# A hybrid decoder block: two more Strassen tiles in another product order, block sums moved into the last loop, GpSimd's order changed

## The chip, the cores and the metric

One core of a Trainium2 chip runs the whole block. The metric is the device time of one execution in microseconds (us), less being better.

## The reference

One decoder block on 512 tokens of width 1024, in float32, cut to what matters here:

```python
h = rmsnorm(x, attn_norm_g)
q, k_c, v_c, k_s, v_s, k_w, v_w, nsa_gate, rwkv_in, gate_a, gate_b = split(h @ w_in)
o_a = nsa_mixer(q, k_c, ..., cmp_w1_k, cmp_w2_k, ...)   # 8 heads; compressed, selected, window branches
o_b = rwkv7_mixer(rwkv_in, ...)                         # 8 heads of 64, a recurrence over the tokens
x = x + (sigmoid(gate_a) * (o_a @ w_proj_a) + sigmoid(gate_b) * (o_b @ w_proj_b)) @ w_out
u = rmsnorm(x, ffn_norm_g) @ w_up                       # 1024 -> 2 * 2816, a gate half and a value half
val, gate = split(conv_b + causal_conv3(u))             # per channel, width 3
x = x + (silu(gate) * val) @ w_down                     # 2816 -> 1024
```

## The kernel before

TensorE multiplies fp32r numbers, and every float32 operand is split into a high and a low part (`hh`, `hl` of the activations; `whi`, `wlo` of a weight, which is loaded to `raw`, rounded by ScalarE to `whi`, and subtracted by VectorE or GpSimd to `wlo`). A product is then three matmuls: hh·whi, hl·whi and hh·wlo.

The program runs through these stages: the input projection; the RWKV recurrence over eight chunks c = 0 to 7, with the key compression of the attention woven into it (TensorE's and GpSimd's order there is that of the code); the attention, whose gaps are filled with tiles of `w_proj_b`; the merge, eight column tiles of `w_proj_a`, one in 2.7 us; `w_out`; the second norm; the FFN up; the FFN down.

**FFN up.** The 22 column tiles f of 128 gate and 128 value columns are either dense (48 matmuls of 512 columns, both halves together) or, for f in `SF` = 3 to 17, done with Strassen's seven products of half size (`up_strassen`): `up_product` is 12 matmuls of 256 columns. Five products use block sums of the input (`R1`, `M2`, `R3`, `Q`) and four of them block sums of the weights (`TS1` to `TS4`). The PSUM banks are `mmb()`, `pa()` and `pb()` (names `ps_mm`, `ps_a`, `ps_b` in the profile). The gate's first half is H11 + H12: each is a product in a bank of its own, ScalarE copies H11 to `us`, and VectorE adds the bank of H12 to it. The convolution `conv` then reads the gate from `cr` in SBUF.

**Sums of weights.** They are made in HBM by DMAs that GpSimd issues: `sums_in_memory` copies rows of `w_up` to `usum` and adds others with an accumulating DMA, one row block k of 128 rows and all columns of `SF` at a time. These have a width of 128 x 15 = 1920 columns (7680 bytes); `max_dma_last_dim=2048` bounds the bytes of one packet, so that the accumulating ones are issued as 128x4x480 (512 packets of 1920 bytes), and a sum of sums as 480x512 (480 packets of 2048 bytes). The copies and adds are started one by one during the recurrence, and the rest when the attention begins. `down_sums` does the same for `w_down` (`dsum`): `down_copy` and `down_add`, each started by `after`, in which GpSimd waits for a named result with a copy to `hold`. All DMAs of GpSimd share one queue, q0 in the profile; SP's weight loads go through q1.

**FFN down.** Strassen as well; the first `PD` = 9 pairs of tiles have their block sums made in `gate_value`, during the FFN up, and `down_tokens` makes the others in steps. In the last, joint loop over g = 0 to 10 the products P4, P5, P7 and P1 run together.

**Keys of the compression.** `kv_proj(1, n)` ends with `norm_keys(1)`, four multiplications `QK<-QK,kss` on GpSimd, which wait for `kss` from VectorE. Behind them in GpSimd's order stand the loads of `spent_load(3, 0)`: the compression weights into buffers that earlier work has used up (`AB`, `BKT`, `AR`).

The lines of the weight loads, `norm_keys` and the spent loads:

```python
def spent_load(s4, a): ...          # AB, BKT, AR <- in_cmp_w_k, on GpSimd's queue
            if c == 1:
                spent_load(3, 0)
            ...
            if c:
                memory_down.send(Xs[0:1, 0, 0:1])    # the next down_copy or pair of down_adds
            if 2 <= c < 7:
                next(memory_sums)                    # the next copy to usum; at the end all adds
```

Of the kernel before, what the change touches and what calls it, by code (L numbers as in the profile page):

```python
# [10 lines left out]
F32 = mybir.dt.float32  # L11
# [21 lines left out]
DOWN_ = [range(g, min(g + 2, NG)) for g in range(0, NG, 2)]  # L33
NCMP = 31
# [4 lines left out]
SF = range(3, 18)  # L39
# [45 lines left out]
def hybrid_block(ctx: ExitStack, tc: tile.TileContext, A: dict, out: bass.AP):  # L85
# [152 lines left out]
    def sums_in_memory(early=5, lead=3):  # L238
        todo = [(t, s_ - e, ij, src) for s_ in range(6)
                for t, e, ij, src in ((TS1, 0, (0, 0), (0, 1)), (TS3, 0, (0, 1), (1, 1)), (TS2, 1, (1, 1), TS1),  # L240
                                      (TS4, 2, (1, 0), TS2)) if 0 <= s_ - e < 4]
        todo[12:14] = todo[13], todo[12]

        def copy(n):
            t, k, ij, _ = todo[n]
            nc.gpsimd.dma_start(usum[t][128 * k:128 * k + 128], up_rows(*ij, k))

        def addition(n):
            t, k, _, src = todo[n]
            nc.gpsimd.dma_start(usum[t][128 * k:128 * k + 128],  # L250
                                up_rows(*src, k) if type(src) is tuple else usum[src][128 * k:128 * k + 128],
                                accum_op=ALU.add, max_dma_last_dim=2048)

        for n in range(early):
            copy(n)
            yield
        for n in range(early - lead):
            addition(n)
        for n in range(early, len(todo) + lead):
            if n == len(todo):  # L260
                yield
            if n < len(todo):
                copy(n)
            addition(n - lead)
# [15 lines left out]
    def down_sums():  # L280
        for g in range(NG):
            after((yield))
            down_copy(g)
        for g in range(0, NG, 2):
            after((yield))
            for g_ in range(g, min(g + 2, NG)):
                down_add(g_)
        while True:
            yield
# [4 lines left out]
    def weight_tiles():  # L294
# [48 lines left out]
        for f in list(SF) + [None]:  # L343
            p = SF[-1] if f is None else f - 1
            if f is not None:
                stream += [up_block(f, 0, 0), up_block(f, 1, 0)]
            if f != SF[0]:
                stream.append(up_sum(p, TS4))
            if f is not None:
                stream.append(up_sum(f, TS2))  # L350
            if f != SF[0]:
                stream.append(up_block(p, 1, 1))
            if f is not None:
                stream += [up_sum(f, TS1), up_sum(f, TS3)]
# [513 lines left out]
    def kv_proj(b, n):  # L868
# [8 lines left out]
        if b == 1:  # L877
            norm_keys(1)
# [64 lines left out]
    with tc.manual_schedule(engines={mybir.EngineType.PE, mybir.EngineType.Pool}):  # L943
        for m in range(NGA):
            act(siga[m], dense_fm(hh, hl))
        below(0)
# [3 lines left out]
        left(0)  # L950
        left(16)
# [179 lines left out]
    with tc.manual_schedule(engines={mybir.EngineType.PE, mybir.EngineType.Pool}):  # L1131
# [7 lines left out]
        for c in range(NCH):  # L1139
# [451 lines left out]
    cr = fp.tile([128, 3, 512], F32, name="cr", tag="d1b")  # L1591
# [45 lines left out]
    def down_tokens():  # L1637
# [23 lines left out]
        for a, b, N, t in tails:  # L1661
# [5 lines left out]
    craw = [cr[:, 0], cr[:, 1], cr[:, 2], cgq[:, 14:16].rearrange("p a n -> p (a n)")]  # L1667
# [30 lines left out]
    def up_strassen():  # L1698
# [4 lines left out]
        for f in list(SF) + [None]:  # L1703
            if f is not None:
                B1 = mmb()[:, b0]
                up_product(B1, H[0][0], True, 1 if f == SF[0] else 2)
                u = [us[:, 3 * (f % 2) + k] for k in range(3)]
                Cg, Cv = craw[f % 2], craw[2 + f % 2]
# [7 lines left out]
            if prev is not None:  # L1716
                urgent.clear()
                f_, B1_, B5_, u_, Cg_, Cv_ = prev
                up_product(B1_, H[1][1])
                act(Cg_[:, b1], B1_)  # L1720
                cg = conv(Cg_, NF + f_, f_ % 2)
            if f is not None:
                up_product(B1, M2)
                act(u[1], B1, AF.Copy, scale=-1.0)
            if prev is not None:
                up_product(B5_, Q)
                stt(Cv_[:, b0], B5_, -1.0, u_[1])
                cv = conv(Cv_, f_, 2 + f_ % 2)
                gate_value(f_, cg, cv)
            if f is not None:  # L1730
                B5 = pb()[:, b0]
                up_product(B5, R1, True)
                up_product(B1, R3)
                act(u[2], B1, AF.Copy, scale=-1.0)
                stt(Cv[:, b1], B5, -1.0, u[2])
                prev = f, B1, B5, u, Cg, Cv
# [123 lines left out]
    with tc.manual_schedule(engines=everything):  # L1860
# [13 lines left out]
        for i, gs in enumerate(DOWN_):  # L1874
# [12 lines left out]
            elif i == 3:  # L1887
                assert next(side, 0) == 0
# [6 lines left out]
            for j, g in enumerate(gs):  # L1895
                product(P1, (a1[:, 0, g], a1[:, 1, g]), [x[:, j] for x in w], g == 0, g == NG - 1)
        u = [[x[:, o + 2 * t:o + 2 * t + 2].rearrange("p a n -> p (a n)") for t in range(2)]
             for x, o in ((cgq, 8), (cgq, 12), (ql, 12))]
# [93 lines left out]
```

## Time and profile before

| | |
|---|---|
| time, median of 3 runs | 800.53 us (799.17 to 800.59) |
| the profiled execution | 801.03 us, of which the span is 799.2 us |
| TensorE busy | 786.7 us, 98% of the span |
| VectorE, ScalarE, GpSimd busy | 633.0, 486.6, 116.0 us (79%, 61%, 15%) |
| DMA | 146.47 MB, mean 183 GB/s; q1 37.1% and q0 27.5% of 16 engines' time |
| the accumulating and copying DMAs into `usum` | 32 issues of 960 KB, about 30 us from issue to landing |

The profiled execution is 1.83 us longer than its span, and 0.50 us above the median. TensorE works nearly all the time, so what counts is how much work it has and where it is made to wait.

### The profile page before, as it was taken

The page shows a single profiled execution, that of the slowest core. Times are in us where ns is not written, and L with a number is a line of the kernel's source. Part 1 is how long each engine was busy: PE and PEld are TensorE (multiplying, and loading weights), DVE is VectorE, ACT ScalarE, POOL GpSimd, SP SyncE. Part 2 cuts the span into 40 slices and gives each one's busy share as a digit, 9 for nine tenths or more (in the row PEclk, how much of TensorE's full clock was granted, in tenths as well). Part 3 has the DMA queues.
Part 4 walks back from the last instruction along what each step waited for, and adds up shares of the span by engine and source line. Part 5 has one row for each costly group of instructions (what it writes and reads, how often), then busy time and mean ns, then how long its engine had stood idle before and what let it go on. Part 6 is the DMA issues. An engine that isn't in the chain of part 4 may idle for free.

```text
span 799.2 us, 14545 instructions
## 1 busy us (share of the span) xinstructions
PE 786.7 (98%) x5547; PEld 672.4 (84%) x5547; DVE 633.0 (79%) x1177; ACT 486.6 (61%) x928; POOL 116.0 (15%) x165
## 2 busy tenths in 40 slices
PE   7999999998999999999999999999999999999998
PEld 5788888886778788788788898999999988888886
DVE  4688899973565588889595489999999999899766
ACT  6777765553355578778444356777777775554442
POOL 5311121153121052120000100000000000003101
PEclk9999999999999999999999999999999999999999
DMA  7554533337999679999857933666666642585753
GB/s 222 152 162 154 178 95 111 80 107 198 208 211 257 192 143 262 273 257 275 213 161 261 198 135 107 198 185 176 192 182 181 184 144 66 164 304 204 251 178 110
DMA packets 149402, 146.47 MB, mean 183 GB/s; under 512 B 6398, under 2 KB 125365, under 8 KB 149205
## 3 DMA queue, kind: packets, MB, share of 16 engines
q1 hardware_dynamic: 128592, 85.57, 37.1%
q0 software_dynamic: 19680, 57.44, 27.5%
q10 hardware_dynamic: 1060, 2.55, 1.0%
q8 instruction: 43, 0.70, 0.4%
q14 instruction: 27, 0.21, 0.1%
HBM read 140.09 MB, written 47.38 MB: 235 GB/s over the span
## 4 chain that ended last, share of the span: by engine, by line
PE 95%; DMA 2%; DVE 1%; ACT 1%; issue 0%; POOL 0%; SPq 0%; DVEq 0%; ACTq 0%; POOLq 0%
PE ps_mm L126 52%; PE ps_mm L1682 11%; PE ps_mm L1798 6%; PE ps_b L1682 5%; PE ps_a L126 5%; PE ps_a L1798 4%; PE ps_b L1798 4%; PE ps_a L1682 3%; PE ps_b L126 2%; PE ps_b L1408 1%; DMA raw<-in_w_in_dram 1%; PE ps_mm L1408 1%; DMA AB<-in_cmp_w_k_dram 1%; DMA kc<-in_consts_dram 1%; PE ps_b L449 0%; ACT whi L129 0%
## 5 line engine op out<-in xcount | busy, mean ns | idle before, releaser
L129 ACT ACTIVATE whi<-raw 128x1024 fp32r<-128x1024 f32 (+2 forms) x153 | 152.7, 998 | 120.9 <-PE ps_mm L126 49.0
L411 DVE TENSOR_TENSOR wlo<-raw,whi 128x1024 fp32r<-128x1024 f32 (+1 forms) x138 | 158.5, 1150 | 43.0 <-ACT whi L129 23.4
L126 PE MATMUL ps_mm<-hh,whi 128*128 128x512 f32 (+1 forms) x384 | 149.2, 392 | 0.3 <-ACT whi L129 0.2
L126 PE MATMUL ps_mm<-hl,whi 128*128 128x512 f32 (+1 forms) x384 | 141.8, 382 | 0.0
L126 PE MATMUL ps_mm<-hh,wlo 128*128 128x512 f32 (+1 forms) x384 | 95.9, 381 | 0.0
L126 PEld LDWEIGHTS ps_mm<-hh,whi 128*128 128x128 f32 x384 | 72.3, 188 | 16.9 <-issue 1.5
L126 PEld LDWEIGHTS ps_mm<-hh,wlo 128*128 128x128 f32 x384 | 72.2, 188 | 14.0
L126 PEld LDWEIGHTS ps_mm<-hl,whi 128*128 128x128 f32 x384 | 70.3, 188 | 13.3 <-DVE hl L141 0.3
L1830 POOL DMA_DIRECT2D cgq<-dsum x6 | 3.2, 541 | 270.2 <-DVE ql L132 234.1
L129 ACT ACTIVATE P<-P,nm 128x512 f32<-128x512 f32 (+3 forms) x64 | 35.3, 554 | 8.0 <-DVE nm L1371 7.9
L141 DVE SCALAR_TENSOR_TENSOR cgq<-cr,cw,cgq 128x511 f32<-128x511 f32 (+1 forms) x44 | 32.9, 747 | 5.0 <-ACT cgq L129 4.5
L1371 DVE CUSTOM_DVE_ANT_0 P<-ps_a,AB 128x512 f32<-128x512 f32 (+3 forms) x64 | 29.4, 483 | 2.1 <-PE ps_a L126 2.1
L1682 PE MATMUL ps_mm<-hl,whi 128*128 128x256 f32 x120 | 30.1, 283 | 0.0
L1682 PE MATMUL ps_mm<-hh,whi 128*128 128x256 f32 x120 | 30.1, 283 | 0.0
L132 DVE TENSOR_TENSOR cgq<-cgq 128x512 f32<-128x512 f32 (+1 forms) x36 | 24.2, 671 | 1.5 <-DMA cgq<-in_w_down_dram 0.9
L1682 PEld LDWEIGHTS ps_mm<-hl,whi 128*128 128x128 f32 x120 | 23.0, 192 | 0.1
L1682 PEld LDWEIGHTS ps_mm<-hh,whi 128*128 128x128 f32 x120 | 23.0, 192 | 0.1
L129 ACT ACTIVATE QK<-ps_mm 128x64 f32<-128x64 f32 (+5 forms) x52 | 13.3, 302 | 15.3 <-PE ps_mm L126 15.3
L126 PE MATMUL ps_mm<-whi,hh 128*128 128x280 f32 (+2 forms) x72 | 22.4, 331 | 0.0
L126 PE MATMUL ps_mm<-whi,hl 128*128 128x280 f32 (+2 forms) x72 | 21.9, 323 | 0.0
L129 ACT ACTIVATE ring<-cgq 128x1024 fp32r<-128x1024 f32 x12 | 12.7, 1059 | 14.8 <-issue 5.4
L141 DVE SCALAR_TENSOR_TENSOR cgq<-ps_mm,cw,cgq 128x511 f32<-128x511 f32 (+1 forms) x28 | 20.3, 741 | 0.2
(544 smaller groups left out, 2022.5 us busy)
## 6 DMA issues: line engine op xcount, KB each, us to landing
usum<-in_w_up_dram POOLq DMA_DIRECT2D x24, 960.0 KB, 30.3
raw<-in_w_in_dram SPq DMA_DIRECT2D x38, 512.0 KB, 5.3
raw<-usum SPq DMA_DIRECT2D x60, 256.0 KB, 3.4
raw<-in_w_up_dram SPq DMA_DIRECT2D x45, 256.0 KB, 3.4
dsum<-in_w_down_dram POOLq DMA_DIRECT2D x22, 512.0 KB, 5.7
raw<-in_w_down_dram SPq DMA_DIRECT2D x20, 512.0 KB, 4.6
usum<-usum POOLq DMA_DIRECT2D x8, 960.0 KB, 27.6
raw<-in_w_up_dram SPq DMA_DIRECT2D x14, 512.0 KB, 3.8
```

Source lines behind the costliest of these rows:

```text
L126: te.matmul(o, lhsT=l, rhs=r, start=start, stop=stop)
L129: sc.activation(o, i, f, **kw)
L132: v.tensor_tensor(o, a, b, op=op)
L141: v.scalar_tensor_tensor(o, a, s, b, op0=op0, op1=op1)
L411: eng.tensor_tensor(lo, raw, hi.bitcast(F32), op=ALU.subtract)
L1371: v.tensor_tensor_reduce(out=P[:, b, r], in0=sp[:, r - r0, b], in1=BT[:, h, 384 - 128 * qt:512], scale=-1.0, scalar=-NEG, op0=ALU.add, op1 ...
L1408: te.transpose(pt[:, 128 * i:128 * i + 128], P[:, x, i, 128 * k:128 * k + 128], ident)
L1682: te.matmul(bank_, lhsT=(hi, lo)[k // 4][:, k % 4], rhs=y[:, k % 4], start=first and k == 0 and y is x[0], stop=k == 7, skip_group_check=n ...
L1798: te.matmul(banks[t], lhsT=x_[:, 128 * t:128 * t + 128], rhs=y, start=first and n == 0, stop=end and n == 2, skip_group_check=more)
L1830: nc.gpsimd.dma_start(raws[g][i], s_)
```

## The change

Three things. (1) `SF` is 3 to 19, 17 tiles in place of 15, and the seven products of a tile are done in another order: H11, then R1 and the H22 of the tile before, M2, H12, Q of the tile before, R3. From the third tile on ScalarE writes H11 into the bank `G`, H12 is accumulated on top of it, and the convolution reads the gate from that bank; VectorE's addition is gone there. `usum` becomes 2176 columns wide. (2) `PD` is 10, and the block sums of the other pairs in `down_tokens` and `two_parts` are made later, partly in the joint loop. (3) GpSimd: `norm_keys(1)` stands after `spent_load(3, 0)`; the first two `down_copy` are started before the recurrence; the additions of `dsum` start singly at first; six copies to `usum` in place of five stand ahead of the attention's bulk.

```diff
-SF = range(3, 18)
+SF = range(3, 20)
+DOWN_SUMS = [[0], [1]] + [range(g, min(g + 2, NG)) for g in range(2, NG, 2)]
...
-    def sums_in_memory(early=5, lead=3):
+    def sums_in_memory(early=6, lead=3):
...
             act(vt[:, t, b], bkv[t][:, 128:256])
             if b == 1:
                 act(gts[:, t], bkv[t][:, 256:280], AF.Tanh, scale=0.5)
-        if b == 1:
-            norm_keys(1)
...
         for m in range(NGA):
             act(siga[m], dense_fm(hh, hl))
+        memory_down.send(siga[0][0:1, 0:1])
         below(0)
...
         left(0)
+        memory_down.send(ABq[0][0:1, 0, 32:33])
         left(16)
...
             if c == 1:
                 spent_load(3, 0)
+                assert next(kv1, 0) == 0
+                norm_keys(1)
...
-            if c:
+            if c > 1:
                 memory_down.send(Xs[0:1, 0, 0:1])
-            if 2 <= c < 7:
+            if c > 1:
                 next(memory_sums)
...
-                act(u[0], B1)
-                B2 = pa()[:, b0]
-                up_product(B2, H[0][1], True)
-                tt(Cg[:, b0], u[0], B2, ALU.add)
+                G = pa()
+
+                on_top = f > SF[0] + 1
+                act(G[:, b0] if on_top else us[:, 4 + f % 2], B1)
...
+                B5 = pb()[:, b0]
+                up_product(B5, R1, True)
+                Cv = craw[f_ % 2]
+                stt(Cv[:, b1], B5, -1.0, u_[1])
                 up_product(B1_, H[1][1])
-                act(Cg_[:, b1], B1_)
-                cg = conv(Cg_, NF + f_, f_ % 2)
+                act(G_[:, b1], B1_)
+                cg = conv(G_, NF + f_, f_ % 2)
             if f is not None:
                 up_product(B1, M2)
-                act(u[1], B1, AF.Copy, scale=-1.0)
+                act(u[0], B1, AF.Copy, scale=-1.0)
+                up_product(G[:, b0], H[0][1], not on_top)
+                if not on_top:
+                    tt(G[:, b0], G[:, b0], us[:, 4 + f % 2], ALU.add)
...
             elif i == 4:
-                two_parts(a2b[:, 0, :, 0], a2b[:, 1, :, 0], cgq[:, 8:14])
+                next(side)
...
-                if g in (2, 4, 6):
-                    k = g // 2 - 1
-                    two_parts(a1[:, 0, k], a1[:, 1, k], q4[k])
-                if g == NG - 2:
+                if g < 3:
+                    next(side)
+                elif g == 3:
+                    assert next(side, 0) == 0
+                    two_parts(a2b[:, 0, :, 0], a2b[:, 1, :, 0], cgq[:, 8:14])
+                elif g == 7:
+                    two_parts(a1[:, 0, 0:3], a1[:, 1, 0:3], ql[:, 0:3])
+                elif g == NG - 2:
                     two_parts(a1[:, 0, 3:7], a1[:, 1, 3:7], ql[:, 3:7])
```

GpSimd's order in the first chunks of the recurrence, where `wlo` are low parts of input weights, `QK` the normed queries and keys, and `AB`, `BKT`, `AR` the spent loads. Before:

```order
L411 TENSOR_TENSOR wlo<-raw,whi 128x840 x2
L411 TENSOR_TENSOR wlo<-raw,whi 128x560
L883 TENSOR_TENSOR QK<-QK,kss 128x128 x4
L956 TENSOR_TENSOR QK<-QK,qss 128x512 x4
L883 TENSOR_TENSOR QK<-QK,kss 128x128 x4
L915 DMA AB<-in_cmp_w_k_dram 128x4x256
L913 DMA BKT<-in_cmp_w_k_dram 128x256 x2
L913 DMA AR<-in_cmp_w_k_dram 128x2x128 x2
L270 COPY hold<-Xs 1x1
L276 DMA dsum<-in_w_down_dram 256x1x512 x2
```

And now:

```order
L412 TENSOR_TENSOR wlo<-raw,whi 128x840
L271 COPY hold<-sg_1716 1x1
L277 DMA dsum<-in_w_down_dram 256x1x512
L412 TENSOR_TENSOR wlo<-raw,whi 128x840
L271 COPY hold<-AB 1x1
L277 DMA dsum<-in_w_down_dram 256x1x512
L412 TENSOR_TENSOR wlo<-raw,whi 128x560
L882 TENSOR_TENSOR QK<-QK,kss 128x128 x4
L957 TENSOR_TENSOR QK<-QK,qss 128x512 x4
L914 DMA AB<-in_cmp_w_k_dram 128x4x256
L912 DMA BKT<-in_cmp_w_k_dram 128x256 x2
L912 DMA AR<-in_cmp_w_k_dram 128x2x128 x2
```

The second four multiplications `QK<-QK,kss` now follow these rows; the spent loads have moved ahead of them, and two transfers of `dsum` with their waits ahead of two of the `wlo`.

GpSimd's order at the start of the attention, where the bulk of the weight sums is issued. Before:

```order
L250 DMA usum<-in_w_up_dram 128x4x480 x2
L246 DMA usum<-in_w_up_dram 128x1920
L250 DMA usum<-in_w_up_dram 128x4x480
L246 DMA usum<-in_w_up_dram 128x1920
L250 DMA usum<-in_w_up_dram 128x4x480
L246 DMA usum<-in_w_up_dram 128x1920
L250 DMA usum<-usum 480x512
```

And now:

```order
L251 DMA usum<-in_w_up_dram 128x8x272 x3
L247 DMA usum<-in_w_up_dram 128x2176
L251 DMA usum<-in_w_up_dram 128x8x272
L247 DMA usum<-in_w_up_dram 128x2176
L251 DMA usum<-usum 544x512
```

An accumulating transfer from `w_up` was cut into 4 packets of 480 columns for each of 128 rows, and is now cut into 8 of 272; one copy more lies ahead of these rows. The rows go on in the same pattern.

## Rows read from the trace of the kernel before

**Rows 1.** The page's chain that ended last, shares of the span.

```profile
PE 95%; DMA 2%; DVE 1%; ACT 1%; issue 0%; POOL 0%; SPq 0%; DVEq 0%; ACTq 0%; POOLq 0%
```

**Rows 2.** Windows: stretch, us, busy PE, PEld, DVE, ACT, POOL, granted clock, DMA, GB/s.

```profile
495.40:643.70 148.30, 148.30 (x1237) 148.30 (x1236) 137.14 (x199) 108.51 (x169) 0.00 (x0) 1.00 0.63 183
720.20:780.00 59.80, 59.80 (x266) 49.51 (x265) 45.91 (x50) 27.36 (x32) 10.97 (x15) 1.00 0.61 207
195.00:200.00 5.00, 4.38 (x20) 2.49 (x21) 0.00 (x0) 0.00 (x0) 1.45 (x2) 0.66 1.06 243
```

**Rows 3.** The chain that ended last: start, us, engine, tile, line, count.

```profile
190.90 4.68 DMA AB<-in_cmp_w_k_dram
...
496.79 1.44 PE ps_a L1682 x12
...
649.29 40.83 PE ps_mm L126 x180
```

**Rows 4.** TensorE's timeline, recurrence: start, us, operation, [idle before and its releaser].

```profile
172.85 0.81 PE L126 MATMUL ps_mm<-wlo,hh 128*128 128x280 f32 x5
...
183.63 0.58 PE L126 MATMUL ps_a<-UV,AB 128*64 128x64 f32 x14
...
195.62 0.46 PE L126 MATMUL ps_mm<-AB,sg 128*64 128x256 f32 x1 [2.44 <-DMA AB<-in_cmp_w_k_dram]
```

**Rows 5.** GpSimd's timeline, the recurrence.

```profile
169.51 1.36 POOL L411 TENSOR_TENSOR wlo<-raw,whi 128x560 fp32r<-128x560 f32 x1 [5.01 <-ACT whi L129]
...
189.48 1.48 POOL L883 TENSOR_TENSOR QK<-QK,kss 128x128 f32<-128x128 f32 x4 [9.65 <-DVE kss L141]
...
194.31 2.14 POOL L276 DMA_DIRECT2D dsum<-in_w_down_dram  x2
```

**Rows 6.** ScalarE's timeline, around 170 us and in the merge.

```profile
170.54 0.59 ACT L129 ACTIVATE AB<-ps_a 32x512 f32<-32x512 f32 x1 [1.94 <-PE ps_b L126]
...
398.40 0.63 ACT L129 ACTIVATE whi<-raw 128x512 fp32r<-128x512 f32 x1 [3.33 <-DMA raw<-in_w_proj_a_dram]
...
400.19 0.63 ACT L129 ACTIVATE whi<-raw 128x512 fp32r<-128x512 f32 x1 [0.63 <-DMA raw<-in_w_proj_a_dram]
```

**Rows 7.** VectorE's timeline, one Strassen tile.

```profile
566.30 0.41 DVE L132 TENSOR_TENSOR cr<-us,ps_a 128x256 f32<-128x256 f32 x1
```

**Rows 8.** VectorE's groups after 640 us: count | busy, mean ns | idle before.

```profile
L132 DVE TENSOR_TENSOR a2b_pairs<-cgq,a2b_pairs 128x1536 fp32r<-128x1536 f32 x1 | 1.8, 1758 | 0.4 <-ACT a2b_pairs L129 0.4
...
L132 DVE TENSOR_TENSOR ql<-ql,a2a_pairs 128x1280 f32<-128x1280 f32 x1 | 1.5, 1485 | 0.0
```

**Rows 9.** DMA queues from 290 to 400 us: packets, MB, share of 16 engines.

```profile
q0 software_dynamic: 8370, 23.73, 89.7%
```

**Rows 10.** The same from 324 to 326 us: accumulating packets alone.

```profile
q0 software_dynamic: 205, 0.42, 113.9%
```

**Rows 11.** The same from 57 to 58 us: plain packets of 512 bytes.

```profile
q1 hardware_dynamic: 634, 0.32, 108.0%
```

**Rows 12.** The same from 413 to 414 us: plain packets of 2048 bytes.

```profile
q1 hardware_dynamic: 185, 0.37, 98.7%
```

**Rows 13.** The same from 384 to 391 us, the first loads of the merge.

```profile
q0 software_dynamic: 531, 1.70, 91.5%
q1 hardware_dynamic: 521, 0.26, 17.1%
```

**Rows 14.** The same from 393 to 400 us.

```profile
q0 software_dynamic: 90, 0.17, 12.8%
```

**Rows 15.** SP's timeline: two issues of merge weights.

```profile
387.04 0.37 SPq L382 DMA_DIRECT2D raw<-in_w_proj_a_dram  x1
...
394.00 0.37 SPq L382 DMA_DIRECT2D raw<-in_w_proj_a_dram  x1
```

**Rows 16.** TensorE's timeline, two of the merge's eight tiles.

```profile
400.33 1.98 PE L126 MATMUL ps_mm<-oaT,whi 128*128 128x512 f32 x8
...
403.05 1.98 PE L126 MATMUL ps_mm<-oaT,whi 128*128 128x512 f32 x8
```

More of the change, by code (lines that the diff above doesn't have):

```diff
@@ L283, in down_sums @@
             down_copy(g)
-        for g in range(0, NG, 2):
+        for gs in DOWN_SUMS:
             after((yield))
-            for g_ in range(g, min(g + 2, NG)):
-                down_add(g_)
+            for g in gs:
+                down_add(g)
         while True:
@@ L345, in weight_tiles @@
             if f is not None:
-                stream += [up_block(f, 0, 0), up_block(f, 1, 0)]
+                stream.append(up_block(f, 0, 0))
             if f != SF[0]:
-                stream.append(up_sum(p, TS4))
+                stream += [up_sum(p, TS1), up_sum(p, TS4)]
             if f is not None:
-                stream.append(up_sum(f, TS2))
+                stream += [up_sum(f, TS2), up_block(f, 1, 0)]
             if f != SF[0]:
@@ L353, in weight_tiles @@
             if f is not None:
-                stream += [up_sum(f, TS1), up_sum(f, TS3)]
+                stream.append(up_sum(f, TS3))
         yield stream[:1], 4, 128, v
@@ L1590, in hybrid_block @@
     R3Q = xr.tile([128, 2, 2, 4, 256], F32R, name="R3Q", tag="x1")
-    cr = fp.tile([128, 3, 512], F32, name="cr", tag="d1b")
+    cr = fp.tile([128, 2, 512], F32, name="cr", tag="d1b")
     us = fp.tile([128, 6, 256], F32, name="us", tag="d3a")
@@ L1660, in down_tokens @@
             yield
-        for a, b, N, t in tails:
             stt(ql[:, a:b], N, -1.0, whole(t[:, 0, 0:b - a, 0]), ALU.mult, ALU.subtract)
@@ L1665, in down_tokens @@
             yield
-    craw = [cr[:, 0], cr[:, 1], cr[:, 2], cgq[:, 14:16].rearrange("p a n -> p (a n)")]
+    craw = [cr[:, 0], cr[:, 1]]
     wpart = []
@@ L1706, in up_strassen @@
                 up_product(B1, H[0][0], True, 1 if f == SF[0] else 2)
-                u = [us[:, 3 * (f % 2) + k] for k in range(3)]
-                Cg, Cv = craw[f % 2], craw[2 + f % 2]
-                act(u[0], B1)
-                B2 = pa()[:, b0]
-                up_product(B2, H[0][1], True)
-                tt(Cg[:, b0], u[0], B2, ALU.add)
+                u = [us[:, 2 * (f % 2) + k] for k in range(2)]
+                G = pa()
+                on_top = f > SF[0] + 1
+                act(G[:, b0] if on_top else us[:, 4 + f % 2], B1)
             else:
@@ L1717, in up_strassen @@
                 urgent.clear()
[L1718 removed]
+                f_, B1_, G_, u_ = prev
+                B5 = pb()[:, b0]
+                up_product(B5, R1, True)
+                Cv = craw[f_ % 2]
+                stt(Cv[:, b1], B5, -1.0, u_[1])
                 up_product(B1_, H[1][1])
[L1720 to L1721 removed]
+                act(G_[:, b1], B1_)
+                cg = conv(G_, NF + f_, f_ % 2)
             if f is not None:
                 up_product(B1, M2)
[L1724 removed]
+                act(u[0], B1, AF.Copy, scale=-1.0)
+                up_product(G[:, b0], H[0][1], not on_top)
+                if not on_top:
+                    tt(G[:, b0], G[:, b0], us[:, 4 + f % 2], ALU.add)
             if prev is not None:
[L1726 to L1728 removed]
+                up_product(B5, Q)
+                stt(Cv[:, b0], B5, -1.0, u_[0])
+                cv = conv(Cv, f_, 2 + f_ % 2)
                 gate_value(f_, cg, cv)
             if f is not None:
[L1731 to L1732 removed]
                 up_product(B1, R3)
[L1734 to L1736 removed]
+                act(u[1], B1, AF.Copy, scale=-1.0)
+                prev = f, B1, G, u
         return run(following)
@@ L1887, in hybrid_block @@
             elif i == 3:
-                assert next(side, 0) == 0
                 two_parts(a2a[:, 0, :, 0], a2a[:, 1, :, 0], ql[:, NG:])
             elif i == 4:
-                two_parts(a2b[:, 0, :, 0], a2b[:, 1, :, 0], cgq[:, 8:14])
+                next(side)
             elif i == 5:
@@ L1897, in hybrid_block @@
         u = [[x[:, o + 2 * t:o + 2 * t + 2].rearrange("p a n -> p (a n)") for t in range(2)]
-             for x, o in ((cgq, 8), (cgq, 12), (ql, 12))]
+             for x, o in ((ql, 12), (cgq, 8), (cgq, 12))]
         P4, P5, P7 = [mmb(), mmb()], [mmb(), mmb()], [pb(), pb()]
```

## The prediction

> **What bounds the kernel now.** I read the chain that ended last first: 95% of it is TensorE [rows 1], so a gain has to take matmuls away or end a wait of TensorE, and a loss has to make it wait. Then the windows, stage by stage. Through the Strassen tiles TensorE works in every one of 148.3 us, with VectorE second at 137.1 us, 92% [rows 2]. In the joint loop it also works all the time, and VectorE 45.9 of 59.8 us [rows 2]. So these two stages are priced by TensorE's own work, and VectorE is what could end that. TensorE's timeline shows two places elsewhere that the change touches. In the recurrence it stands idle for 2.44 us until `AB` has come in [rows 4]. In the merge nothing stands still, but the weights arrive just in time: ScalarE waits 3.33 and 0.63 us for two of them [rows 6], and TensorE takes them 1.4 and 2.3 us after ScalarE began [rows 16]. Last I read the queues, because GpSimd's queue q0 is full at 89.7% from 290 to 400 us [rows 9] and runs out just in the merge.
>
> **The change, part by part.**
>
> *The spent loads.* The load of `AB` is issued at 190.90 and takes 4.68 us [rows 3], because GpSimd stands before it in the multiplications of `norm_keys(1)`, which waited 9.65 us for `kss` and began at 189.48 [rows 5]. The last reader of the old `AB` is done at 183.63 + 0.58 = 184.2 [rows 4]. With the loads ahead of the multiplications, the load can go out at about 184.2 and be there at 184.2 + 4.7 = 188.9. TensorE came to it at 195.62 − 2.44 = 193.18, so the whole 2.44 us go. Behind the idle time the granted clock is 0.66 over 5 us [rows 2], between its levels of 1.2 and 2.4 GHz: 5 × 0.34 = 1.7 us more. Together −4.1 us, bounds −2.4 (the clock falls anyhow) and −4.1. What is late next is `norm_keys(1)` by 3 us of issues; its keys are for the attention, 100 us later.
>
> *Two more Strassen tiles.* A product is 1.44 us, and the dense tiles behind the Strassen ones are 180 matmuls in 40.83 us, 0.227 each [rows 3]. A dense tile of 48 is 10.89 us, a Strassen tile 7 × 1.44 = 10.08. Two tiles: −1.6 us. The order of the products takes no matmul away. The addition that goes is 0.41 us of VectorE [rows 7]: of some 9.3 us a tile (137.1 / 14.7 tiles in the window) 8.9 are left in 10.08. VectorE isn't waited for there, so this is worth nothing by itself. ScalarE's write into the bank lies a whole product ahead of its use.
>
> *Block sums into the joint loop.* The pieces that come in are about two of 1.49 us and one of 1.76 [rows 8]: 4.7 us, and 45.9 + 4.7 = 50.6 of 59.8. TensorE covers them: 0. The upper bound is a piece of 1.76 + 1.49 in front of one that TensorE needs, +3.2.
>
> *The early transfers of `dsum`.* They stand ahead of low parts of weights. The second waits for `AB` from ScalarE, done at 170.54 + 0.59 = 171.13 [rows 6]. With 0.2 us for the hold, 1.07 for the issue (2.14 for two) and 1.36 for the subtraction behind it, which began at 169.51 [rows 5], the low part is ready at 173.8. TensorE's five matmuls on these begin at 172.85 [rows 4], and the third part is wanted near 173.3. So +0.5 us, bounds 0 and +0.9.
>
> *The queue of the weight sums.* This is the largest term. An accumulating packet of 2048 bytes takes 16 × 2 us × 1.139 / 205 = 178 ns [rows 10]. From `w_up` they had 1920 bytes, 512 of them a transfer, 32 on each of 16 engines; now they have 1088 bytes, and there are 64 on each engine. No row shows an accumulating packet of 1088 bytes. Plain ones take 16 × 1.08 / 634 us = 27 ns at 512 bytes [rows 11] and 16 × 0.987 / 185 = 85 ns at 2048 [rows 12]. A straight line between these gives 81 and 49 ns at 1920 and 1088, so of 178 ns I estimate 168 and 102. Eight such transfers are issued at the attention: 8 × 64 × 102 − 8 × 32 × 168 = +9.2 us. Five sums of sums have 34 packets an engine in place of 30: 5 × 4 × 178 = +3.6. Ten copies of longer rows in place of eleven: +0.8. Together +13.6 us. The lower bound is the price by bytes alone, 95 ns: +10.1. The upper one is the same 168 ns for each packet, +47. I take the straight line, since the plain rows show that price follows size.
>
> The Trainium skill, page "DMA: Bandwidth & Descriptors", section "Why small descriptors are slow (HBM only)", states a fixed overhead of about 3 cycles for each packet beside its beats of 32 bytes. By that, 1920 and 1088 bytes are 63 and 37 cycles, so an estimate of 168 × 37 / 63 = 99 ns and +11.9 us in place of +13.6, on the same side.
>
> *What the queue delays.* From 393 to 400 us q0 has only 12.8% of 7 us left, 0.9 us [rows 14]; so it ends at about 394, and then at 394 + 13.6, about 407. From 384 to 391 us q0 and q1 got 531 and 521 packets through [rows 13]: one for one, so that the small packets of a weight load each wait for a big one. The load issued at 387.04 [rows 15], 32 packets an engine, was there only at 398.40 [rows 6], after 11.3 us; the next, issued at 394.00, when q0 was empty, came at 400.19. Now the second meets q0 too. It is there after as long as the first, 394.0 + 11.3 = 405.3, or when the queue ends, near 406. TensorE wants its high part at 403.05 [rows 16], ScalarE takes 0.63 us [rows 6], so it must land by 402.4: 2.9 to 3.6 us late. I take 3.6. The load behind it on q1 is wanted one tile later and adds between 0 and 3.6; I take 2.2, since q0 is empty for part of it. That is 5.8 us of idle time, in two pieces, and 1.7 us for the clock as at 195 us: +7.5 us. Bounds: 0, if q0 ends before 400, and 12 to 18 at 168 ns (below). What comes later isn't touched: the next weights are plain loads without q0.
>
> **The sum.** 801.03 − 4.1 − 1.6 + 0 + 0.5 + 7.5 = 803.3 us for the profiled execution. It was 0.5 above the median, so 802.8.
>
> **Rivals.**
>
> *The loads still land in time.* q0 was not busy all the time: 89.7% of 110 us are 98.7 us [rows 9], in about 104 to its end, so about 5 us could take up work. With that, and 95 ns a packet, the overrun is 10.1 − 5 = 5 us, q0 ends at 399, and the load issued at 394 is there by 402. That decides it: the end of q0 before or after 400 to 401. Then 801.03 − 4.1 − 1.6 + 0.5 − 0.5 = 795.3, up to 798 with a wait of under 3 us. Against it: the shares over 100% in [rows 10] say that the engines were as full as they get while sums ran.
>
> *Each accumulating packet has one price.* If reading, adding and writing cost a fixed turn whatever the size, q0 has 47 us more and goes on to 440. All five last loads of the merge then take turns with it: 32 × (168 + 27) ns = 6.2 us each for tiles of 2.72 [rows 16], 3.5 us late each, 17.5 together, less up to 5 that the buffers run ahead. 12 to 18 us and the clock: 795.3 + 1.7 + 12 to 18 = 809 to 815. For it: the accumulating packet takes twice the plain one, so something other than bytes counts. Against it: none of the plain rows.
>
> *VectorE becomes the bound in the joint loop.* It decides when its share there passes about 95%, or when a sum of 1.49 us stands ahead of a weight's low part: +3.2 and 1.7 of clock on the 795.3, about 800.
>
> *The wait in the recurrence stays.* Something else that TensorE needs at 193 us (`raw`, `sg`) is no earlier than 195.6, and the change doesn't do what it says there: 4.1 us more than the forecast, 806.9. Against it: the timeline names the DMA of `AB` alone.
>
> **How the numbers follow.** The forecast (the merge waits for 4 to 8 us) has 0.43, with a range of its own of 800 to 806; the loads in time 0.32; one price 0.13; VectorE 0.06; the wait stays 0.06. 0.2% is 1.6 us, about what a measurement of this kernel can tell from no change. Faster, below 798.9: 0.30 of the loads in time, 0.04 of the forecast's lower edge and 0.02 of VectorE, 0.36. Within 798.9 to 802.1: 0.17 of the forecast and 0.04 of the others, 0.21. Slower: 0.43. The range of 795 to 811 leaves out the upper half of the one price (0.06) and what is better than 795.3 by the runs' spread, some 0.07.
>
> **What would show it.** TensorE has no idle time before `AB` at 193 us, and the granted clock there is 1. q0's packets are near 102 ns in the attention, and q0 ends near 407. In the merge `whi` waits for its load at the fourth and fifth of the late tiles, and TensorE behind it, with a lower clock afterwards. A Strassen tile is still 10.08 us with no idle time. The prediction is wrong if q0 ends before 400 or after 420, if TensorE waits at g = 0 to 7 of the joint loop, or if the low part near 173 us costs over 1 us.

## The result and the profile after

The changed kernel takes 806.03 us (median of 6 runs, 804.87 to 807.68), against 800.58 of the kernel before: the ratio is 1.0071, with an interval of 1.0056 to 1.0086. So it is slower, by 0.7%, and 3.2 us above the forecast of 802.8. The profiled execution took 806.02 us, its span is 804.2. The executions of the kernel before lie in two groups 1.8 us apart by their mean granted clock, as told below under the spent loads, so its median moves with their mix.

TensorE's waits in the changed kernel, from the view of waits (us in total, times, longest):

```profile
PE ps_b L450 <- DMA kc<-in_consts_dram: 4.8, 1, 4.8
PE ps_mm L127 <- ACT whi L130: 4.1, 2, 3.9
PE ps_mm L1684 <- ACT us L130: 1.0, 1, 1.0
PE ps_mm L127 <- POOL wlo L412: 0.9, 1, 0.9
PE ps_mm L1684 <- ACT whi L130: 0.7, 1, 0.7
PE ps_mm L1803 <- DVE wlo L412: 0.7, 1, 0.7
```

The wait for `AB` of [rows 4] is gone. Five waits are new or longer: the second to the sixth row. (Of the second, 3.86 us lie in the merge; the other 0.20 us stand at the start of the FFN, where the kernel before has 0.21 as well.) Where the time went is read by the starts of the same work in the two chains that ended last. Of the kernel before:

```profile
203.26 2.94 PE ps_mm L126 x12
...
387.03 65.20 PE ps_mm L126 x306
...
473.29 22.07 PE ps_mm L126 x96
...
705.24 14.96 PE ps_a L1798 x66
```

Of the changed kernel:

```profile
200.19 2.94 PE ps_mm L127 x12
...
383.98 5.27 PE ps_mm L127 x42
...
390.95 12.26 DMA raw<-in_w_proj_a_dram
...
476.36 22.06 PE ps_mm L127 x96
...
692.29 1.41 DVE ql L142
693.72 1.27 DVE ql L133
...
710.38 14.96 PE ps_a L1803 x66
```

The recurrence is 3.07 us ahead and stays so until the attention's end (383.98 for 387.03). Behind the merge it is 3.07 behind (476.36 for 473.29), so the merge costs 6.14. Behind the FFN up it is 5.14 behind (710.38 for 705.24), so the FFN, which was to gain 1.6, loses 2.07. From there on the two run alike.

The merge, in TensorE's and ScalarE's timelines, in the windows and in the queues of the changed kernel. TensorE's late tile, and the weight that ScalarE waited for:

```profile
404.00 2.60 PE L127 MATMUL ps_mm<-oaT,whi 128*128 128x512 f32 x8 [3.86 <-ACT whi L130]
```

```profile
403.32 0.63 ACT L130 ACTIVATE whi<-raw 128x512 fp32r<-128x512 f32 x1 [6.88 <-DMA raw<-in_w_proj_a_dram]
```

The windows from 400 to 410 us and from 690 to 715 us, columns as in [rows 2]:

```profile
400.00:410.00 10.00, 6.14 (x20) 4.45 (x20) 4.49 (x8) 3.46 (x6) 0.00 (x0) 0.83 0.64 145
690.00:715.00 25.00, 24.31 (x107) 19.43 (x106) 24.74 (x29) 13.65 (x16) 1.08 (x2) 1.00 0.70 233
```

GpSimd's queue from 290 to 400 us:

```profile
q0 software_dynamic: 12258, 25.04, 100.2%
```

From 290 to 300 us, where nearly all of its packets are accumulating ones of 1088 bytes:

```profile
q0 software_dynamic: 1544, 1.66, 107.5%
```

From 393 to 400 us:

```profile
q0 software_dynamic: 499, 1.78, 91.3%
```

And from 400 to 405 us:

```profile
q0 software_dynamic: 289, 0.57, 61.6%
```

In place of [rows 14], where q0 is all but empty after 393 us, it is full until 400 and has 5 × 0.616 = 3.1 us of work left then; its last packets come at 406. The load that TensorE waits for was issued at 390.95 and took 12.26 us, and the granted clock behind the wait is 0.83 over 10 us, 1.7 us lost.

### The profile page after: what moved, and what is told of

It reads as the page before. It is cut to its first block, busy times and chain, and to the rows that moved or that the text cites. A ratio compares the mean times of both kernels' runs of the same rounds, so it can differ in the third digit from the quotient of the medians.

```text
span 804.2 us, 14710 instructions
## 1 busy us (share of the span) xinstructions
PE 787.8 (98%) x5619; PEld 675.4 (84%) x5619; DVE 638.3 (79%) x1165; ACT 490.0 (61%) x935; POOL 118.4 (15%) x166
## 4 chain that ended last, share of the span: by engine, by line
PE 94%; DVE 2%; DMA 2%; ACT 1%; issue 0%; POOL 0%; DVEq 0%; ACTq 0%; POOLq 0%; SPq 0%
PE ps_mm L127 49%; PE ps_mm L1684 12%; PE ps_b L1684 6%; PE ps_mm L1803 5%; PE ps_a L127 5%; PE ps_a L1803 4%; PE ps_b L1803 3%; PE ps_a L1684 3%; PE ps_b L127 2%; DMA raw<-in_w_proj_a_dram 2%; PE ps_b L1411 1%; PE ps_mm L1411 1%; ACT whi L130 1%; DVE wlo L412 1%; DMA kc<-in_consts_dram 1%; PE ps_b L450 0%
## 5 line engine op out<-in xcount | busy, mean ns | idle before, releaser
L412 DVE TENSOR_TENSOR wlo<-raw,whi 128x1024 fp32r<-128x1024 f32 (+1 forms) x141 | 162.3, 1152 | 41.7 <-ACT whi L130 25.9
L127 PE MATMUL ps_mm<-hh,whi 128*128 128x512 f32 (+1 forms) x352 | 136.6, 392 | 0.3 <-ACT whi L130 0.2
L127 PE MATMUL ps_mm<-hl,whi 128*128 128x512 f32 (+1 forms) x352 | 129.4, 381 | 0.0
L127 PE MATMUL ps_mm<-hh,wlo 128*128 128x512 f32 (+1 forms) x352 | 88.0, 380 | 0.0
L127 PEld LDWEIGHTS ps_mm<-hh,wlo 128*128 128x128 f32 x352 | 66.2, 188 | 12.7
L1684 PE MATMUL ps_mm<-hh,whi 128*128 128x256 f32 x136 | 34.2, 284 | 0.7 <-ACT whi L130 0.7
L1684 PE MATMUL ps_mm<-hl,whi 128*128 128x256 f32 x136 | 34.1, 283 | 0.0
L142 DVE SCALAR_TENSOR_TENSOR cgq<-cr,cw,cgq 128x511 f32<-128x511 f32 (+1 forms) x34 | 25.5, 750 | 6.8 <-ACT cgq L130 6.2
L142 DVE SCALAR_TENSOR_TENSOR cgq<-ps_a,cw,cgq 128x511 f32<-128x511 f32 (+1 forms) x34 | 25.3, 745 | 2.4 <-ACT cgq L130 2.0
L1684 PE MATMUL ps_mm<-hh,wlo 128*128 128x256 f32 x136 | 22.0, 284 | 0.0
```

The lines of the kernel that those rows point to most:

```text
L127: te.matmul(o, lhsT=l, rhs=r, start=start, stop=stop)
L142: v.scalar_tensor_tensor(o, a, s, b, op0=op0, op1=op1)
L412: eng.tensor_tensor(lo, raw, hi.bitcast(F32), op=ALU.subtract)
L1684: te.matmul(bank_, lhsT=(hi, lo)[k // 4][:, k % 4], rhs=y[:, k % 4], start=first and k == 0 and y is x[0], stop=k == 7, skip_group_check=n ...
```

## The experiments

Medians are of the runs of one kernel; the kernel before had 799.4 to 800.9 us beside them, and the ratio is to that.

**1. The packets of the sums, cut at 2176 bytes.**

```diff
-                                accum_op=ALU.add, max_dma_last_dim=2048)
+                                accum_op=ALU.add, max_dma_last_dim=2176)
```

> The changed kernel with the accumulating transfers into the up sums cut at 2176 bytes in place of 2048: 128x4x544 for 128x8x272, as many bytes in half the packets. Theory (the wait of 3.9 us in the merge comes from the small packets that fill GpSimd's queue): packets of about 190 ns where two of 107 ns stood, 8 x 32 x 190 = 48.6 us for 8 x 64 x 107 = 54.8 us, so the queue ends 6 us earlier, at 397; TensorE's idle time before oaT,whi falls from 3.9 to under 1 us, and the time from 806.0 to 800 to 802 us. Rival (the bytes of the wider sums alone): the queue ends where it did and the time stays at 805 to 807. Rival (the merge waits for something else, such as coming 3 us earlier to loads that were just in time): also 805 to 807, with the queue's end earlier.

Measured: 805.48 us, ratio 1.0062 (1.0046 to 1.0079). From 290 to 300, from 290 to 400, and from 400 to 405 us its queue had:

```profile
q0 software_dynamic: 845, 1.80, 100.8%
...
q0 software_dynamic: 8225, 25.48, 95.8%
...
q0 software_dynamic: 79, 0.14, 15.5%
```

The packet of 2176 bytes takes 16 × 10 × 1.008 / 845 = 191 ns, the one of 1088 took 16 × 10 × 1.075 / 1544 = 111. Half the packets save engine time as expected: 290 to 405 us hold 105.4 + 0.8 = 106.2 us of q0, for 110.2 + 3.1 = 113.3 in the changed kernel and 98.7 before [rows 9]. But the queue still works until 400, with its last packets at 402 to 403, about 3 us earlier than in the changed kernel. The last sum is issued only 3.2 us earlier, since GpSimd waits for a copy to land before it issues it. The changed kernel, then this run:

```profile
378.65 1.02 POOL L251 DMA_DIRECT2D usum<-usum  x1 [15.61 <-DMA usum<-in_w_up_dram]
...
375.47 1.01 POOL L251 DMA_DIRECT2D usum<-usum  x1 [14.67 <-DMA usum<-in_w_up_dram]
```

The merge's load takes 11.68 us for 12.26: TensorE waits three times, 0.61, 0.34 and 1.72 us, and loses the clock as well. So the time falls by 0.5 us where 4 to 6 were expected. The theory's number was wrong, and the rival that the bytes decide is nearly right for the time: of 14.6 us that the queue got more, 7.5 stay when a packet is a whole row of 2176 bytes.

**2. The norm of the keys back ahead of the spent loads.**

```diff
+        if b == 1:
+            norm_keys(1)
...
                 spent_load(3, 0)
-                assert next(kv1, 0) == 0
-                norm_keys(1)
```

> The changed kernel with the norm of the second half's compressed keys back ahead of the spent loads on GpSimd. Theory: TensorE waits for AB near 194 us again, 2.4 us and a halved clock behind it, so 4 us slower than the changed kernel, 810 us; unless the merge, which is reached 4 us later, then waits that much less, since the queue of the sums starts later too by the same time: no change there expected. Rival (the recurrence is bound elsewhere, the wait only moves): 806.

Measured: 809.17 us, ratio 1.0110 (1.0091 to 1.0129). TensorE waits again:

```profile
196.72 0.43 PE L127 MATMUL ps_mm<-AB,sg 128*64 128x256 f32 x1 [2.25 <-DMA AB<-in_cmp_w_k_dram]
```

That is 3.1 us slower than the changed kernel by the medians, 4 were expected, and the wait has its old place and size. The clock behind it is the difference. The windows of this kernel behind the wait:

```profile
195.00:200.00 5.00, 3.28 (x22) 2.24 (x23) 0.59 (x2) 0.41 (x2) 0.30 (x1) 1.00 0.88 268
200.00:205.00 5.00, 5.00 (x50) 3.99 (x49) 2.23 (x5) 1.82 (x3) 0.00 (x0) 1.00 0.37 102
```

The granted clock stays at 1 behind 2.25 us of idle time, where it fell to 0.66 behind 2.44 us in [rows 2]. It doesn't stay there in every execution of this kernel: three of the six, the profiled one among them, took 807.8 to 808.3 us at a mean granted clock of 0.998, and three took 810.0 to 810.6 at 0.995 or 0.996, which is about the 4 us that were expected.

**3. The two early transfers of the down sums left out** (they go back into the chunks).

```diff
-DOWN_SUMS = [[0], [1]] + [range(g, min(g + 2, NG)) for g in range(2, NG, 2)]
+DOWN_SUMS = [range(g, min(g + 2, NG)) for g in range(0, NG, 2)]
...
-        memory_down.send(siga[0][0:1, 0:1])
...
-        memory_down.send(ABq[0][0:1, 0, 32:33])
...
-            if c > 1:
+            if c:
                 memory_down.send(Xs[0:1, 0, 0:1])
```

> The changed kernel without the two early transfers of the down sums, which go back into the chunks of the recurrence. Theory: GpSimd's low part near 172 us is in time, TensorE's 0.9 us wait and what the clock lost behind it go, 1.1 us faster: 805. Rival (the transfers then stand in the full queue before the attention and push its end out, so the merge waits longer): 806 to 808.

Measured: 805.35 us, ratio 1.0064 (1.0047 to 1.0081), 0.7 less than the changed kernel. The wait for `wlo` of GpSimd is no longer in the view of waits, and the merge still waits, 3.6 us. The theory holds, a little smaller.

**4. The kernel before with the GpSimd edit alone.** The reverse of the diff of 2, in the kernel before.

> The kernel before with one edit of the change: the norm of the second half's compressed keys behind the spent loads. Theory: the wait of 2.44 us for AB goes and the granted clock stays at 1 behind it, 4.1 us faster: 796.4 us, ratio 0.995. Rival (the merge is then too early for its loads): the gain shrinks to 1 to 2 us.

Measured: 797.49 us, ratio 0.9965 (0.9954 to 0.9975); in a second set of runs (12 below) 797.49 again. In its chain the row that stood at 203.26 starts 4.15 us earlier, the one at 387.03 is 3.51 us earlier:

```profile
199.11 2.94 PE ps_mm L126 x12
...
383.52 65.19 PE ps_mm L126 x306
```

So the term of 4.1 is right where it was worked out; 0.6 of it is given back in the next chunk, where TensorE waits 0.2 us for VectorE's `UV`. Reaching the merge earlier brings no wait there.

**5. Sums for 15 tiles only.** Tiles 18 and 19 take the sums of tiles 3 and 4, so their columns are not the reference's; TensorE's work is the same.

```diff
-    usum = dp.tile([4, 512, 128 * len(SF)], F32, name="usum")
+    usum = dp.tile([4, 512, 128 * 15], F32, name="usum")
...
-        o = 128 * (f - SF[0])
+        o = 128 * ((f - SF[0]) % 15)
...
-        return A["w_up"][0][512 * i + 128 * k:512 * i + 128 * k + 128, o:o + 128 * len(SF)]
+        return A["w_up"][0][512 * i + 128 * k:512 * i + 128 * k + 128, o:o + 128 * 15]
```

> The changed kernel with sums of weights for 15 tiles alone, 1920 columns as before; tiles 18 and 19 take the sums of tiles 3 and 4, so these two columns are not the reference's. TensorE's work is unchanged. Theory (the merge waits for the bytes that the wider sums put into GpSimd's queue): the queue ends near 392, the idle time of 3.9 us before oaT,whi and the clock lost behind it go, 6.1 us faster than the changed kernel: 800. Rival (TensorE comes 3 us earlier to loads that are no earlier): a wait of 2 to 3 us stays, 803.

Measured: 800.16 us, ratio 1.0004 (0.9995 to 1.0013): 5.9 less than the changed kernel, and no wait of TensorE in the merge. From 290 to 400 us the queue has:

```profile
q0 software_dynamic: 8144, 22.61, 86.2%
```

It is empty by 390. So the wider sums are the cause of the wait in the merge.

**6. The last copy and the addition behind it held back** until the second norm.

```diff
-            if n == len(todo):
+            if n == len(todo) - 1:
                 yield
```

> The changed kernel with the last copy of the sums and the addition behind it held back until the second norm, with the three additions that already are. Theory: 7 to 8 us of work leave GpSimd's queue ahead of the merge, it ends near 396, the idle time in the merge falls from 3.9 to under 1 us: 800 to 801. Rival (the sums now come too late for the first Strassen tile, or delay w_up's loads): a new wait of 1 to 4 us between 470 and 500 us, 802 to 805.

Measured: 800.20 us, ratio 1.0001 (0.9992 to 1.0010). No wait in the merge, and none for the sums later: this one line, which holds back one copy and one addition, gives back 5.8 us.

**7. Three repairs in the FFN.**

```diff
-                stream += [up_sum(f, TS2), up_block(f, 1, 0)]
+                stream += [up_sum(f, TS2), up_block(f, 1, 0)][::-1 if f == SF[0] else 1]
...
-            else:
-                following = dense_fm_g(hh, hl)
-                next(following)
...
                 stt(Cv[:, b1], B5, -1.0, u_[1])
+                if f is None:
+                    following = dense_fm_g(hh, hl)
+                    next(following)
...
+                if f == SF[0]:
+                    up_product(G[:, b0], H[0][1], True)
                 up_product(B1, M2)
                 act(u[0], B1, AF.Copy, scale=-1.0)
-                up_product(G[:, b0], H[0][1], not on_top)
+                if f > SF[0]:
+                    up_product(G[:, b0], H[0][1], not on_top)
...
-        for _ in range(2):
+        for _ in range(2 if f < NF - 1 else 1):
             next(side)
...
-            if i > 1:
+            if i > 0:
                 next(side, None)
```

> The changed kernel with three repairs in the FFN: in the first Strassen tile H12 goes ahead of M2, so that M2 doesn't follow H11 into the bank that ScalarE is emptying; behind the last tile R1 goes ahead of the dense matmuls, so that ScalarE has 2.7 us for the weights of H22; at tile 21 one step of the block sums in place of two goes to VectorE, the other steps one place later. Theory: the three waits of 0.99, 0.72 and 0.69 us go with the clock lost behind each, 3.7 us: 802.3. Rival (one of them moves on to the next weight or bank): 0.5 to 1.3 us less gained for each.

Measured: 804.65 us, ratio 1.0063 (1.0048 to 1.0077), 1.4 less where 3.7 were expected. One repair of three works: the wait behind the last tile is gone. The two others moved on. TensorE's timeline has these now:

```profile
503.52 1.22 PE L1684 MATMUL ps_mm<-R3Q,whi 128*128 128x256 f32 x8 [0.94 <-ACT us L130]
...
700.65 0.72 PE L1806 MATMUL ps_mm<-wlo,a2b_pairs 128*128 128x512 f32 x2 [0.32 <-DVE wlo L412]
...
704.20 0.73 PE L1806 MATMUL ps_mm<-wlo,a2b_pairs 128*128 128x512 f32 x2 [0.51 <-DVE wlo L412]
```

In the first tile R3 now follows M2 into the bank. Three of its four products go there, since R1 was put off to the next tile and there is no tile before it to work on; one fourth product can't part three.

**8. 3, 6 and 7 together.**

> The changed kernel with the held sums, the three repairs of the FFN and the late transfers of the down sums together. Theory (the losses are those four and add up): 806.0 - 6.1 - 3.7 - 0.7 = 795.5, below the kernel before with the one edit on GpSimd (797.5). Rival (the gain of the two more tiles is eaten up elsewhere): 797.5 or more.

Measured: 798.36 us, ratio 0.9979 (0.9969 to 0.9989). The measured gains add up (806.03 − 5.83 − 0.68 − 1.38 = 798.14), but the two waits that moved on are still there, and it isn't under the 797.49 of run 4.

**9. 3, 6 and the repairs of 7 but for its last line, with two more:** in the first tile R1 in its own turn, and the last subtraction of each group of block sums on GpSimd.

```diff
+                else:
+                    B5 = pb()[:, b0]
+                    up_product(B5, R1, True)
...
-            yield
-            tt(ql[:, a:b], ql[:, a:b], whole(t[:, 1, 0:b - a, 0]), ALU.subtract)
+            nc.gpsimd.tensor_tensor(ql[:, a:b], ql[:, a:b], whole(t[:, 1, 0:b - a, 0]), op=ALU.subtract)
             yield
```

> The changed kernel with the held sums and the late down transfers of the run before, R1 ahead of the dense matmuls behind the last tile, and two new repairs: in the first tile R1 stays in its own turn, between M2 and R3, so that no product follows another into the bank that ScalarE empties; the last subtraction of each of the two groups of block sums goes to GpSimd, which takes 1.49 us from VectorE in the down stage and 1.49 in the joint loop. Theory (the bank of the first tile, and VectorE being full from 690 to 715 us, are what is left of the loss): neither 0.94 us near 497 nor 0.32 and 0.51 near 695 us, 2.2 us with the clock, 796.2, under the kernel before with the one edit on GpSimd (797.5). Rival (VectorE's next piece is late instead, or GpSimd's subtraction slows VectorE): a wait of 0.5 to 1.5 us between 690 and 760 stays, 797 to 798.5.

Measured: 798.67 us, ratio 0.9985 (0.9976 to 0.9994). The bank is repaired: TensorE has no idle time from 485 to 700 us. GpSimd's part is the rival's case, in TensorE's and in GpSimd's timeline:

```profile
708.15 0.73 PE L1808 MATMUL ps_a<-wlo,a 128*128 128x512 f32 x2 [1.54 <-DVE wlo L413]
```

```profile
699.47 6.94 POOL L1664 TENSOR_TENSOR ql<-ql,a2a_pairs 128x1280 f32<-128x1280 f32 x1 [4.12 <-DVE ql L142]
```

GpSimd takes 6.94 us for what VectorE does in 1.49 [rows 8], and in the same time one of VectorE's additions, of 512 columns, takes 3.32 us and ends at 706.96, just behind GpSimd's 706.41, where the one ahead of it takes 0.69:

```profile
703.64 3.32 DVE L133 TENSOR_TENSOR cgq<-cgq 128x512 f32<-128x512 f32 x1
```

The low part that TensorE waits for stands right behind this addition.

**10. 3 and 6, with the old order of the products** in all 17 tiles, the gate's addition on VectorE again (`up_strassen` and its stream of weights as before, three rows of `cr`).

> The changed kernel with the held sums and the late down transfers, and the 17 tiles done in the order of products of before, with the gate's addition on VectorE (block sums as changed). Theory (TensorE sets the pace of a tile in either order; the new order itself brings nothing and costs the two waits at the ends of the Strassen tiles): no idle time at 495 to 675 us, only the wait near 690 stays, 806.0 - 5.8 - 0.7 - 2.5 = 797.0. Rival (with the addition VectorE doesn't keep up through 17 tiles, and the new order is needed): waits for wlo in the tiles or behind them, 798 or more.

Measured: 796.79 us, ratio 0.9962 (0.9948 to 0.9976). From 495 to 660 us:

```profile
495.00:660.00 165.00, 165.00 (x1377) 165.00 (x1376) 152.30 (x222) 120.74 (x187) 0.00 (x0) 1.00 0.64 186
```

TensorE never waits, with VectorE at 152.3 of 165 us, 92% as before. The addition that the new order saves wasn't needed, and the new order alone had brought the waits at both ends of the Strassen tiles. Near 688 us 0.53 us are left, a wait for a low part behind a piece of the block sums.

**11. Run 10 with one step of the block sums taken from tile 21** and given back late in the down stage.

```diff
-        for _ in range(2):
+        for _ in range(2 if f < NF - 1 else 1):
             next(side)
...
             elif i == 5:
+                next(side)
                 add_to(0, 0, P2)
```

> The run with the old order of the products, and one step of the block sums taken from VectorE at tile 21 and given back eight products before the joint loop. Theory (VectorE's 1.49 us there is what the down stage's first low part waits for): the wait of 0.53 us near 688 and the clock behind it go, 796.8 - 1.0 = 795.8. Rival (VectorE is full through the whole down stage, so the wait moves on): 796.3 to 797.

Measured: 795.73 us, ratio 0.9944 (0.9929 to 0.9958). TensorE's waits are those of the start and the 0.2 us at the start of the FFN that the kernel before has too:

```profile
PE ps_b L450 <- DMA kc<-in_consts_dram: 5.2, 1, 5.2
PE ps_mm L459 <- DVE h L137: 0.8, 1, 0.8
PE ps_mm L127 <- ACT whi L130: 0.2, 1, 0.2
```

It beats both kernels, the one before by 0.6%.

**12. Run 4 once more, beside run 11.**

> The kernel before with the one edit on GpSimd once more, on the same chip as the run beside it, to see whether the two more Strassen tiles are worth anything once their waits are gone: by the terms 797.5 here, 1.6 us above the run beside it if its last wait goes, 0.7 if it stays.

Measured: 797.49 us, ratio 0.9966 (0.9955 to 0.9978). Run 11 is 1.76 us faster on the same chip, its slowest run (795.97) under the fastest here (797.0). The two chains show where: from the start of the FFN to the products `ps_a` of the FFN down. Run 11, then this run:

```profile
469.73 22.05 PE ps_mm L127 x96
...
700.08 14.96 PE ps_a L1799 x66
...
470.20 22.06 PE ps_mm L126 x96
...
702.18 14.96 PE ps_a L1798 x66
```

That is 230.35 us for 231.98, 1.63 less. The two tiles are worth their 1.6 us once nothing waits for them.

## Why the prediction was right, and where its steps were off

The sign and the largest term were right, and the range held the time; but it is 16 us wide, and most of the rivals' times lie in it too. The point was 2.7 us low for the profiled execution (803.3 for 806.02) and 3.2 for the median, since the 0.5 us between the two didn't carry over. Two terms set to nothing cost 3.7 us, and the merge, forecast 1.4 too dear, hid part of that: so the point is nearer than its terms.

| term | forecast, us | measured, us | from |
|---|---|---|---|
| spent loads | −4.1 | −4.15 | the chain of run 4 at 200 us; here −4.15 + 1.1 = −3.05, for −3.07 |
| early `dsum` | +0.5 | +1.1 by the chain, +0.7 by run 3 | |
| the merge | +7.5 | +6.14 by the chain, 5.8 and 5.9 by runs 6 and 5 | |
| two Strassen tiles | −1.6 | −1.63 by the chain, −1.76 by the medians | runs 11 and 12 |
| the new order of products | 0 | +2.5 | the chain and runs 7, 9, 10 |
| block sums moved | 0 | +1.2 by the chain, +1.06 by run 11 | |

The sum of the measured terms of the FFN is what the chain shows: −1.6 + 2.5 + 1.2 = 2.1, for 2.07.

*The spent loads.* Right in size for the profiled execution. But the clock's 1.7 us don't come with every execution: run 2 has the wait without the fall, and the kernel before has both. Of its 72 executions beside the experiments, 37 took 798.9 to 799.8 us at a mean granted clock of 0.999 or 1, and 35 took 800.5 to 802.9 at 0.997 or 0.998; the 20 of runs 4 and 12, without the wait, have 0.999 or 1. So this edit alone (797.49) is worth 3.6 us against the median of the 35 (801.1) and 1.8 against that of the 37 (799.3), and the forecast started from an execution like the 35 (801.03 at 0.998). That the fall lies at this wait is seen in one profile, and what decides it is not shown.

*The early transfers.* The mechanism was right, in GpSimd's timeline of the changed kernel:

```profile
171.21 0.17 POOL L271 COPY hold<-AB 1x1 f32<-1x1 f32 x1 [4.74 <-ACT AB L130]
171.69 1.08 POOL L277 DMA_DIRECT2D dsum<-in_w_down_dram  x1 [0.31 <-issue]
172.33 1.85 POOL L412 TENSOR_TENSOR wlo<-raw,whi 128x560 fp32r<-128x560 f32 x1
```

The size was off: the subtraction took 1.85 us, not the 1.36 of [rows 5], so the low part came at 174.2 and TensorE waited 0.87. The prediction named over 1 us here as a sign of being wrong: it is 1.1 by the chain, and 0.7 by run 3, where TensorE waits for `UV` as in run 4.

*The queue.* The forecast of 102 ns for a packet of 1088 bytes and of +13.6 us of work stand beside 111 ns and 113.3 − 98.7 = +14.6 us. The Trainium skill, page "DMA: Bandwidth & Descriptors", section "Why small descriptors are slow (HBM only)", gave by its 3 cycles a packet an estimate of 99 ns, which is lower than the 111 measured. The same rule makes two packets of 1088 bytes 2 × 37 / 71 = 1.04 of one of 2176, an estimate; measured are 2 × 111 / 191 = 1.16. The end of the queue, reckoned from the work left in it as the forecast reckoned its 394, was off: near 403, not 407. It starts 3 us earlier, with the kernel, and is fuller, 100.2% for 89.7%, so part of the work went into gaps, as the rival of the loads in time had it; not enough for its case. TensorE waited 3.86 us for the first late load, 3.6 were forecast. The second wait, put at 2.2, didn't come, and the clock cost 1.7, as forecast. With 3.86 + 1.7 = 5.6 the merge is explained to 0.6 us. One reading of the prediction was off, with nothing in the sum hanging on it: TensorE took the two weights 1.9 and 2.9 us after ScalarE began on them, not 1.4 and 2.3 [rows 6, rows 16].

*The new order, the step that failed.* The prediction said that ScalarE's write lies a whole product ahead of its use, and that the order takes and gives nothing. That holds inside the tiles, which take 10.08 us each as forecast, and not at their ends. In the first tile there is no work of a tile before it to lie between H11 and M2, and both use one bank. ScalarE's timeline of the changed kernel shows what M2 waited for:

```profile
499.46 1.06 ACT L130 ACTIVATE whi<-raw 128x1024 fp32r<-128x1024 f32 x1
500.43 0.36 ACT L130 ACTIVATE us<-ps_mm 128x256 f32<-128x256 f32 x1
```

The copy out of the bank stands behind a rounding of weights, and TensorE is idle for 0.99 us. Behind the last tile H22 follows R1 at once, and the weights of H22 are rounded into a buffer only when R1 has read it: 0.72 us.

```profile
670.49 1.06 ACT L130 ACTIVATE whi<-raw 128x1024 fp32r<-128x1024 f32 x1 [0.63 <-PE ps_b L1684]
```

Each costs more than its idle time. From H11 to H12 of the first tile pass 4.12 us, where two products of 1.44 take 2.88, so the first wait costs 1.24 (0.15 lie between the earliest start of M2 and the end of the matmul ahead of it, from which idle time is counted, and 0.10 in M2's first eight matmuls, 1.22 for 1.12):

```profile
498.26 0.28 PE L1684 MATMUL ps_mm<-hh,whi 128*128 128x256 f32 x1
...
502.38 0.28 PE L1684 MATMUL ps_a<-hh,whi 128*128 128x256 f32 x1
```

From R1 (669.29) to Q (673.44) pass 4.15, so the second costs 1.27; together they are the 2.5. The expectation of run 7 added time for the clock, but the clock didn't fall: the window over the first wait has 1.00, as has every window of 5 us from 470 to 760 us.

```profile
500.00:505.00 5.00, 4.16 (x34) 4.16 (x35) 4.66 (x8) 2.64 (x5) 0.00 (x0) 1.00 0.67 188
```

Runs 7 and 9 took one and both away, run 10 had neither.

*The block sums.* VectorE as the bound was a rival, with the joint loop as its place. The joint loop had no wait. The place was the down stage ahead of it, where two pieces of 1.48 and 1.49 us, at 692.29 and 693.72 in the chain, stand ahead of a low part. VectorE has 24.7 of 25 us there, 24.5 in run 10. Run 7 moved one piece by one place within that stage, and waits came up behind it; run 11, in the old order of products, moved it out to the stage's end, and none was left. That VectorE is full there isn't the whole of it: it is as full in run 11, without a wait. What counts is what stands ahead of a low part.

*The rivals.* One price for each packet is out (111 and 191 ns). The loads in time would have been so with 15 tiles' bytes (run 5). The wait in the recurrence did not stay.

Open: why experiment 1 moved the queue's end by only 3 us for the 7 us of engine time that it saved. GpSimd's wait for a copy to land sets when the last sum is issued, 3.2 us earlier there; why the copies landed no earlier isn't shown. Larger packets also make each weight packet beside them wait longer, which would go that way, but no run parts the two.

## What to carry to other kernels

When data made in the background grow, work out when their queue runs empty and which loads of another queue stand beside its end; holding back one copy and one addition of a full queue was worth more here (5.8 us) than making its packets larger (0.5).

When a software pipeline's order is changed, go through its first and its last turn by hand: work that is put off to the next turn is missing as cover in the first, and what covers a buffer's refill in the middle may not be there at the end.

An engine at 92% needn't be relieved if nothing waits for it, and one at 99% can still be without harm: look at which piece stands ahead of the one that TensorE needs.

## What the runs showed of the hardware

The granted clock fell to 0.66 over 5 us behind 2.44 us of idle TensorE [rows 2] and to 0.83 over 10 us behind 3.86 us, and stayed at 1 behind 2.25 us in the profile of run 2; by the mean clock of whole executions it fell in about half of those of the kernel before (35 of 72). Behind waits of 0.69 to 0.99 us in the FFN it stayed at 1. A subtraction of 1280 columns took GpSimd 6.94 us in the down stage beside a full VectorE and 3.32 in the joint loop, where VectorE's own take 1.49; beside the first, an addition of 512 columns took VectorE 3.32 us for 0.69. An accumulating packet of a full queue took 111 ns at 1088 bytes and 191 at 2176.
